# First layer's queries, keys and values of a decoder trunk: one projection in nine chunk pairs, transposed afterwards

## The chip, the core and the metric

One core of one Trainium2 chip runs the whole program. The metric is the device time of one execution in microseconds (us), median of the runs. PE is TensorE (matrix products; PEld its weight loads), DVE is VectorE, ACT is ScalarE, POOL is GpSimd, SP is SyncE, which issues the weight transfers.

## The reference, cut to what matters

The trunk has two layers of different kind, 256 tokens, width 2048, all in float32. What the change touches is the first layer's mixer: 24 heads in three dilation groups (8 columns of heads `j`, three groups `g` each), and four heads that attend to a memory.

```python
def mixer_a(u, mem_n, w_in, w_mem_kv, w_out):
    B, S, _ = u.shape                                # 1, 256, 2048
    na = len(DIL_GROUPS) * A_HEADS_PER_GROUP         # 3 * 8
    proj = u @ w_in                                  # 9216 columns of q, k, v and 512 of mq
    qkv = proj[..., :3 * na * HEAD_DIM].reshape(B, S, 3, na, HEAD_DIM)
    mq = proj[..., 3 * na * HEAD_DIM:].reshape(B, S, MEM_HEADS, HEAD_DIM)
    o_dil = dilated_attention(qkv[:, :, 0], qkv[:, :, 1], qkv[:, :, 2])
    o_mem = memory_attention(mq, mem_n, w_mem_kv)
    return jnp.concatenate([o_dil.reshape(B, S, -1), o_mem.reshape(B, S, -1)], axis=-1) @ w_out

def swiglu(u, w_gu, w_down):
    gu = u @ w_gu
    return (jax.nn.silu(gu[..., :D_FF]) * gu[..., D_FF:]) @ w_down

for l in range(DEPTH):                               # rmsnorm around each part
    x = x + rmsnorm(mixer(rmsnorm(x, g[0])), g[1])   # mixer_a, then mixer_b
    x = x + rmsnorm(swiglu(rmsnorm(x, g[2]), ffn_w_gu[l], ffn_w_down[l]), g[3])
```

The softmax of a head `j` runs over the keys of its three groups together, with a linear bias by distance.

## The kernel before

**Arithmetic.** Every float32 operand is kept as two parts, `hi` (what the matrix engine takes) and `lo` (the rest), and a product is `hi*hi + lo*hi + hi*lo`. Weights arrive by DMA as `raw` (units of 512 KB, two k-tiles of 512 columns or eight of 128), ACT copies `hi` (line 258), DVE subtracts `lo` (line 259). Activations lie transposed, 16 k-tiles `xT` of 128 features by 256 tokens, both parts side by side.

**Forms of a projection.** In the w-form (`w_unit`, `w_mm`) a 128x128 block of weights is stationary and the tokens stream: one matmul of 512 columns (weight `hi` against both parts, line 390) and one of 256 (weight `lo`, lines 389 and 392) for each k-tile. The result is transposed, features by tokens, as queries and keys are needed. In the x-form (`x_unit`, `x_mm`) the tokens are stationary and the weights stream, three matmuls of the chunk's width; the result is tokens by features, as values are needed.

**Seven products.** `Block7` computes a pair of chunks (2 x 512 columns) for both token tiles. A normal k-pair costs 24 matmuls of 512 columns: step `a` for the first chunk and step `b` for the second, 12 each. A k-pair of kind `S` forms sums of the weights on DVE (steps `T13`, `T24`; lines 274, 275, 284, 285) and uses sums of the activations (`Sx`, `Ex`, made once by `x_sums`), and costs 7 x 3 = 21. The products P1 to P7 are put together by additions on DVE (`add`, line 509). Before, the feed-forward chunks of both layers run in this way, in `gu_pair` and in `dn`.

**The stage that the change rewrites.** For each head column `j` of eight there are six w-form projections (queries and keys of three groups, units `a_qk`, evacuated by `evac_w`, lines 417 to 419: two parts added, times the token norm) and one x-form of 384 columns (`a_v`, lines 425 to 427). Then `a_head` is spawned.

**What sets the order.** Each engine runs its own queue in the order in which the code issues. The main stream of matmuls calls `tick()` after each; at a tick one of the side generators (`spawn`) issues its next piece, and `yield n` puts it off for n ticks. `a_head`, `mem_head`, `x_sums` and the evacuations are such generators, so the `yield` numbers fix where their instructions stand among the main ones. `take` looks ahead by `st["look"]` weight units, keeping `st["res"]` pages free: 4 and 0 in this stage, 5 and 5 in the pairs. `a_head` makes scores (line 704), softmax (709 to 717), nine transposes (727, 734), the product with the values (744, 746), and `put_o` (612, 613), which splits the result into the input `oT` of the output projection.

## Time and profile before

| | us |
|---|---|
| runs, median of 3 | 2511.36 (2510.72 to 2513.29) |
| profiled execution, its own time | 2510.36 |
| its span in the profile | 2508.6 |
| PE busy | 2464.3 (98%) |
| DVE busy | 1975.7 (79%) |
| ACT busy | 1360.5 (54%) |
| queries, keys, values and heads of the first layer | 87.4 to 528.9 |
| output projection of the first mixer | 528.9 to 599.5 |
| first feed-forward layer, first matrices | 625 to 1104 |

Busy time counts what an engine executes; matmuls overlap in it, so the time that one takes in the stream is read from one start to the next. The span ends with the last instruction, and the execution's time includes 1.8 us around it.

### The profile page before, as it was taken

The numbers are of one execution on the slowest core, as the hardware profiler recorded it, in microseconds if no ns is written. First come the engines' busy times: TensorE is split into PE (matmuls) and PEld (weight loads), VectorE is DVE, ScalarE is ACT, GpSimd is POOL, SyncE is SP. The second block draws the span as 40 slices with busy tenths as digits, with TensorE's granted clock in tenths as the row PEclk, the third lists the DMA queues.
The fourth block names the chain that finished last, engine by engine and source line by source line (L and its number), as shares of the span: only waits on it lengthen the run. The fifth ranks groups of instructions, "written<-read, shape, count | busy, mean of one in ns | idle before, by whom it ended". The sixth has DMA issues, their size and how long they took to land.

```text
span 2508.6 us, 33084 instructions
## 1 busy us (share of the span) xinstructions
PE 2464.3 (98%) x12050; PEld 2084.8 (83%) x12050; DVE 1975.7 (79%) x2820; ACT 1360.5 (54%) x1984; POOL 76.6 (3%) x106
## 2 busy tenths in 40 slices
PE   8999999999999999999999999999899999999998
PEld 6899999988888888778888888888778888878886
DVE  8555555557798989898897866895689989899796
ACT  7443444446565556565565556565455555555553
POOL 5000000000000000000000000000000000000000
PEclk9999999999999999999999999999999999999999
DMA  7555555576576655476586566346556656458664
GB/s 280 182 179 172 173 164 171 170 252 219 192 252 209 220 170 194 165 252 221 200 291 206 213 247 211 112 150 226 183 186 222 229 177 209 164 171 286 210 221 151
DMA packets 143140, 508.07 MB, mean 203 GB/s; under 512 B 16224, under 2 KB 16352, under 8 KB 142976
## 3 DMA queue, kind: packets, MB, share of 16 engines
q1 hardware_dynamic: 134208, 476.24, 54.8%
q0 software_dynamic: 8048, 28.61, 3.2%
q8 instruction: 94, 1.54, 0.2%
q10 hardware_dynamic: 720, 1.11, 0.1%
q14 instruction: 70, 0.57, 0.1%
HBM read 491.21 MB, written 14.68 MB: 202 GB/s over the span
## 4 chain that ended last, share of the span: by engine, by line
PE 87%; DVE 7%; ACT 3%; issue 2%; DMA 0%; POOL 0%; SPq 0%; DVEq 0%; ACTq 0%; POOLq 0%
PE bk L467 16%; PE bk L465 16%; PE bk L466 16%; PE bk L390 12%; PE bk L392 6%; PE bk L426 5%; PE bk L427 5%; PE bk L425 5%; DVE lo L259 3%; ACT hi L258 2%; PE sk L1068 1%; PE sk L704 1%; PE bk L1407 1%; PE bk L1406 1%; DVE x L814 0%
## 5 line engine op out<-in xcount | busy, mean ns | idle before, releaser
L259 DVE TENSOR_TENSOR lo<-raw,hi 128x1024 fp32r<-128x1024 f32 (+2 forms) x899 | 1043.7, 1205 | 202.9 <-ACT hi L258 188.7
L258 ACT ACTIVATE hi<-raw 128x1024 fp32r<-128x1024 f32 (+2 forms) x899 | 884.3, 1034 | 90.7 <-DVE raw L285 28.4
L390 PE MATMUL bk<-xT,hi 128*128 128x512 f32 x1104 | 399.3, 405 | 0.0
L465 PE MATMUL bk<-hi,xf 128*128 128x512 f32 x780 | 308.2, 395 | 0.0
L467 PE MATMUL bk<-lo,xf 128*128 128x512 f32 x780 | 304.6, 391 | 0.0
L466 PE MATMUL bk<-hi,xf 128*128 128x512 f32 x780 | 304.3, 390 | 0.0
L392 PE MATMUL bk<-xT,lo 128*128 128x256 f32 x1035 | 289.8, 280 | 0.0
L258 ACT ACTIVATE hi<-t 128x1024 fp32r<-128x1024 f32 x92 | 97.7, 1062 | 278.4 <-DVE t L275 258.6
L390 PEld LDWEIGHTS bk<-xT,hi 128*128 128x128 f32 x1104 | 204.1, 188 | 40.0 <-issue 0.2
L465 PE MATMUL bk<-hi,hT 128*128 128x512 f32 x576 | 224.5, 390 | 0.0
L467 PE MATMUL bk<-lo,hT 128*128 128x512 f32 x576 | 224.1, 389 | 0.0
L466 PE MATMUL bk<-hi,hT 128*128 128x512 f32 x576 | 224.1, 389 | 0.0
L392 PEld LDWEIGHTS bk<-xT,lo 128*128 128x128 f32 x1035 | 195.5, 189 | 3.2
L467 PEld LDWEIGHTS bk<-lo,xf 128*128 128x128 f32 x780 | 146.8, 188 | 31.2
L466 PEld LDWEIGHTS bk<-hi,xf 128*128 128x128 f32 x780 | 147.1, 189 | 29.5
L465 PEld LDWEIGHTS bk<-hi,xf 128*128 128x128 f32 x780 | 147.2, 189 | 29.2
L467 PEld LDWEIGHTS bk<-lo,hT 128*128 128x128 f32 x576 | 108.1, 188 | 22.5
L465 PEld LDWEIGHTS bk<-hi,hT 128*128 128x128 f32 x576 | 108.1, 188 | 22.3
L466 PEld LDWEIGHTS bk<-hi,hT 128*128 128x128 f32 x576 | 108.1, 188 | 22.3
L259 DVE TENSOR_TENSOR lo<-t,hi 128x1024 fp32r<-128x1024 f32 x92 | 112.0, 1218 | 0.0
L418 DVE TENSOR_TENSOR ev<-bk,ev 128x256 f32<-128x256 f32 x93 | 39.3, 422 | 91.7 <-ACT ev L417 90.9
L417 ACT ACTIVATE ev<-bk 128x256 f32<-128x256 f32 x93 | 35.6, 382 | 130.4 <-PE bk L390 130.2
(303 smaller groups left out, 4376.9 us busy)
## 6 DMA issues: line engine op xcount, KB each, us to landing
raw<-in_gu SPq DMA_DIRECT2D x352, 512.0 KB, 4.6
raw<-in_dn SPq DMA_DIRECT2D x176, 512.0 KB, 4.5
raw<-in_a_qk SPq DMA_DIRECT2D x96, 512.0 KB, 3.2
raw<-in_a_v SPq DMA_DIRECT2D x64, 384.0 KB, 3.1
raw<-in_cw SPq DMA_DIRECT2D x32, 512.0 KB, 4.6
raw<-in_b_out SPq DMA_DIRECT2D x32, 512.0 KB, 3.6
raw<-in_a_out SPq DMA_DIRECT2D x24, 512.0 KB, 3.8
raw<-in_b_q SPq DMA_DIRECT2D x24, 512.0 KB, 3.2
```

The source lines that it names most:

```text
L258: nc.scalar.activation(hi, src, AF.Copy)
L259: nc.vector.tensor_tensor(out=lo, in0=src, in1=hi.bitcast(F32), op=OP.subtract)
L390: mm(pt[:, :], lhsT=hi[:, ks], rhs=X.hl(kt), start=first, stop=last)
L392: mm(pt[:, S:], lhsT=lo[:, ks], rhs=X.part(kt, 0), start=False, stop=False)
L417: nc.scalar.activation(t1, pt[1][:, S:], AF.Copy)
L418: nc.vector.tensor_tensor(out=t1, in0=pt[1][:, :S], in1=t1, op=OP.add)
L425: mm(p[:, :w], lhsT=xh, rhs=u[0][1][:, ws], start=f, stop=False)
L426: mm(p[:, :w], lhsT=xl, rhs=u[0][1][:, ws], start=False, stop=False)
L427: mm(p[:, :w], lhsT=xh, rhs=u[1][1][:, ws], start=False, stop=l)
L465: mm(p, lhsT=xh, rhs=wh, start=f, stop=False)
L466: mm(p, lhsT=xl, rhs=wh, start=False, stop=False)
L467: mm(p, lhsT=xh, rhs=wl, start=False, stop=e)
```

## The change

The 9216 columns of queries, keys and values become one x-form projection `a_in`, in 18 chunks of 512, in nine pairs by `Block7`, with three `S` k-pairs and five normal ones in each. Its columns are ordered by head: three blocks of 128 for the queries, three for the keys, three for the values. What `gu_pair` did is moved into a common `x_pair`, which the feed-forward calls with its own closing part (`after`); its order of work is as before. After each pair, `a_after` scales the results on ACT by the token norm (values straight into their place, queries and keys in place), transposes the 128x128 pieces of queries and keys on PE, four at most in a group, and copies them on ACT to `aq` and `ak`; when a head's last value block is there, it spawns `a_head`. `x_sums` is issued during the memory queries. `a_head` takes one PSUM bank at a time, and banks are given back six ticks later (`later`).

```diff
+A_PAIRS = 9
+A_QUADS = range(3)
@@ the list of weight units
-    for j in range(AH):
-        u += [("a_qk", j * 12 + i) for i in range(12)]
-        u += [("a_v", j * 8 + i) for i in range(8)]
+    u += _a_order()
@@ x_pair, the common part of gu_pair
+    def x_pair(name, plan, X, Sx, Ex, end, after):
...
+        def evac():
+            yield 10
+            (s1, u2), (u3, v) = T["c"]
+            blk.add("P2", s1, s1)
+            blk.add("P5", v, u3, False)
+            blk.add("P5", u2, u2)
+            yield 1
+            blk.add("P4", u3, u3)
+            blk.add("P3", u2, u2)
+            yield from after(T["c"])
@@ a_head
-            bk = yield from sbank(1 + t)
...
+            for gs in ((0, 1, 2),) if t == 0 else ((0, 1), (2,)):
+                (sb_, s), = yield from sbank()
+                for i, g in enumerate(gs):
+                    mm(s[:, i * n:(i + 1) * n], lhsT=q[1][:, g, t * P:(t + 1) * P], rhs=k[1][:, g, :n], start=True, stop=True)
+                yield 3
...
+                later(sb_)
+                yield 1
@@ put_o and the transposes of a_head
-        banks.put(b)
+        later(b)
@@ the mixer's stage
+    Sx, Ex = {}, {}
+    spawn(x_sums(Xu, Sx, Ex))
     for h in range(4):
         pt = proj_w("a_mq", Xu)
         if h == 0:
-            drain()
+            until(lambda: "R" in rx)
...
+    def a_after(cp):
+        def run(c):
+            tr, done = [], []
+            for i in range(2):
...
+                    for t in range(2):
+                        x, r = c[t][i][:, n * P:(n + m) * P], rx["rs" if kd == 0 else "r"][:, t:t + 1]
+                        nc.scalar.activation(e[kd][1][:, t, g * P:(g + m) * P] if kd == 2 else x, x, AF.Copy, scale=r)
...
+                yield 3
+            yield 4
+            while tr:
+                now, tr = tr[:2], tr[2:]
+                (b, p), = yield from sbank()
+                for f, (_, _, i, n) in enumerate(now):
+                    for t in range(2):
+                        nc.tensor.transpose(p[:, f * S + t * P:f * S + (t + 1) * P], c[t][i][:, n * P:(n + 1) * P], ident)
+                yield 2
...
+                later(b)
+                yield 2
+            for j in done:
+                spawn(a_head(j, *(hd[j][kd] for kd in range(3)), O, 4 + j))
+    for cp in range(A_PAIRS):
+        if cp == 2:
+            until(lambda: O.done.issuperset(range(4)))
+            free_mem(0)
+        x_pair("a_in", _x_steps(A_QUADS), Xu, Sx, Ex, cp == A_PAIRS - 1, a_after(cp))
```

Lines of the changed kernel are shifted: `lo` is line 273 there, the weight sums 288 to 299, `put_o` 712 and 713, `add` 523, the pair's matmuls 479 to 481, a head's value product 840 and 842, the scaling 1075, the transposes 1088.

**The order on VectorE around a head's end.** Before, `put_o` (`oT`) of a head stands among the weight splits and the evacuation (`ev`) of a projection:

```order
L259 TENSOR_TENSOR lo_2526<-raw_2400,hi_2525 128x1024
L259 TENSOR_TENSOR lo_2565<-raw_2422,hi_2564 128x1024
L613 TENSOR_TENSOR oT_624<-sk_2584,oT_624 128x256
L418 TENSOR_TENSOR ev_2595<-bk_2524,ev_2595 128x256
L419 TENSOR_TENSOR aq_2392<-ev_2595,Rs 128x256
L259 TENSOR_TENSOR lo_2601<-raw_2473,hi_2600 128x1024
L259 TENSOR_TENSOR lo_2623<-raw_2502,hi_2622 128x1024
```

In the changed kernel, at the border from one pair to the next, `put_o` of a head is followed by weight splits, the five rows of a seven-product k-pair (`hl`, `t`, `raw`) with its `lo`, and the additions `ut`, of which the first three of five are shown:

```order
L713 TENSOR_TENSOR oT_623<-sk_2087,oT_623 128x256
L273 TENSOR_TENSOR lo_2097<-raw_2015,hi_2096 128x1024
L273 TENSOR_TENSOR lo_2103<-raw_2033,hi_2102 128x1024
L273 TENSOR_TENSOR hl_2120<-raw_2039,hl_2120 128x512
L288 TENSOR_TENSOR t_354_2123<-raw_2039,raw_2033 128x512
L289 TENSOR_TENSOR t_354_2123<-raw_2039 128x512
L298 TENSOR_TENSOR raw_2033<-t_354_2123,raw_2033 128x512
L299 TENSOR_TENSOR raw_2033<-raw_2033 128x512
L273 TENSOR_TENSOR lo_2143<-t_354_2123,hi_2142 128x1024
L523 TENSOR_TENSOR ut_2057<-bk_1707,ut_2057 128x512
L523 TENSOR_TENSOR ut_2058<-bk_1821,ut_2058 128x512
L523 TENSOR_TENSOR ut_2057<-bk_1821,ut_2057 128x512
```

What reads the value product of a head is now ahead of the additions in the same queue.

**The order on PE at the same place.** Before, a head's value product (`apT`, `apU` against `av`) stands between main matmuls, and nothing on PE reads a result of that time soon after:

```order
L392 MATMUL bk_2022<-xT_16_96,lo_1917 128x256
L744 MATMUL sk_2082<-apT_2037,av_1390 128x256 x3
L746 MATMUL sk_2082<-apU_2038,av_1390 128x128 x3
L389 MATMUL bk_2022<-xT_16_96,lo_1917 128x256
L390 MATMUL bk_2022<-xT_16_96,hi_1916 128x512
```

In the changed kernel the value product of that head is followed by 45 main matmuls (two shown at either end) and then by the first group of transposes, which read the sums `ut`:

```order
L840 MATMUL sk_2087<-apT_2044,av_1392 128x256 x3
L842 MATMUL sk_2087<-apU_2045,av_1392 128x128 x3
L479 MATMUL bk_1817<-hi_1999,ex_1090 128x512
L480 MATMUL bk_1817<-hi_1999,ex_1090 128x512
...
L480 MATMUL bk_2128<-hi_2035,xT_14_94 128x512
L481 MATMUL bk_2128<-lo_2036,xT_14_94 128x512
L1088 MATMUL sk_2184<-cst,ut_2057 128x128
L1088 MATMUL sk_2184<-cst,ut_2058 128x128
L1088 MATMUL sk_2184<-cst,ut_2057 128x128
L1088 MATMUL sk_2184<-cst,ut_2058 128x128
```

The transposes are new on PE, and they stand at a fixed distance behind the value product.

**The order on VectorE in the memory queries' stage.** Before, a memory head's maximum (`nm`) and reciprocal (`rec`) stand among `put_o` of another head, weight splits and the evacuations of queries:

```order
L259 TENSOR_TENSOR lo_834<-raw_701,hi_833 128x1024
L259 TENSOR_TENSOR lo_863<-raw_723,hi_862 128x1024
L627 TENSOR_REDUCE nm<-sk_874 128x2
L636 RECIPROCAL rec<-den 128x2
L638 TENSOR_SCALAR mp_882<-mp_882,rec 128x256 x2
L613 TENSOR_TENSOR oT_621<-sk_893,oT_621 128x256
```

In the changed kernel the rows of `x_sums` (`sv`, `xw`, `sx`) stand between:

```order
L677 TENSOR_TENSOR sv<-xw_766 128x128
L678 TENSOR_TENSOR sv<-sv,xw_766 128x128
L679 TENSOR_TENSOR sv<-xw_766 128x128
L680 TENSOR_TENSOR sv<-xw_766,sv 128x128
L684 TENSOR_TENSOR sx_794<-sv,sx_794 128x4x128
L273 TENSOR_TENSOR lo_812<-raw_660,hi_811 128x1024
L673 TENSOR_TENSOR xw_830<-xT_12_92 128x512
L727 TENSOR_REDUCE nm<-sk_834 128x2
L689 TENSOR_TENSOR sv<-xw_830 128x256
L713 TENSOR_TENSOR oT_621<-sk_853,oT_621 128x256
L736 RECIPROCAL rec<-den 128x2
```

The same steps of a memory head are on this engine's queue, with six or seven rows of `x_sums` between one head's and the next.

## Rows read from the trace of the kernel before

**Rows 1.** The page: busy time of each engine with its share of the span and its count of instructions, and the chain of work that ended last, by engine.

```profile
PE 2464.3 (98%) x12050; PEld 2084.8 (83%) x12050; DVE 1975.7 (79%) x2820; ACT 1360.5 (54%) x1984; POOL 76.6 (3%) x106
...
PE 87%; DVE 7%; ACT 3%; issue 2%; DMA 0%; POOL 0%; SPq 0%; DVEq 0%; ACTq 0%; POOLq 0%
```

**Rows 2.** The table by stretches, one for each of the eight heads of the stage that is rewritten (first, last and sum). Columns: stretch and length in us, then busy us (count) of PE, PEld, DVE, ACT, POOL, the granted PE clock, DMA share, GB/s.

```profile
87.40:142.60 55.20, 55.20 (x316) 50.36 (x316) 30.60 (x46) 24.08 (x41) 0.00 (x0) 1.00 0.52 172
...
473.69:528.87 55.18, 55.18 (x323) 50.61 (x323) 30.85 (x45) 24.22 (x37) 1.67 (x3) 1.00 0.60 198
sum 441.47, PE 441.47 PEld 404.69 DVE 246.66 ACT 193.63 POOL 1.67; mean PE 55.18 PEld 50.59 DVE 30.83 ACT 24.20 POOL 0.21
```

**Rows 3.** The timeline of PE in one head: a head's small matmuls and the main matmul that resumes behind each. Columns: start in us, duration, engine, line, out<-in, sizes, count (a float32 matmul leaves two records).

```profile
201.08 0.83 PE L704 MATMUL sk<-ak,aq 128*128 128x128 f32 x6
201.66 0.47 PE L390 MATMUL bk<-xT,hi 128*128 128x512 f32 x1
201.98 0.28 PE L392 MATMUL bk<-xT,lo 128*128 128x256 f32 x1
...
204.18 1.46 PE L704 MATMUL sk<-ak,aq 128*128 128x256 f32 x6
205.29 0.58 PE L390 MATMUL bk<-xT,hi 128*128 128x512 f32 x1
...
212.42 0.49 PE L727 MATMUL sk<-cst,ap 128*128 128x128 f32 x3
212.66 0.48 PE L390 MATMUL bk<-xT,hi 128*128 128x512 f32 x1
...
217.28 1.46 PE L744 MATMUL sk<-apT,av 128*128 128x256 f32 x6
...
219.16 0.36 PE L389 MATMUL bk<-xT,lo 128*128 128x256 f32 x1
```

**Rows 4.** The table by stretches, for one of the middle pairs of the first feed-forward layer (columns as in rows 2); the pair ahead of it and the two behind it differ by 0.01 at most in length and PE.

```profile
787.22:829.64 42.42, 42.42 (x193) 35.14 (x192) 38.65 (x48) 23.64 (x30) 1.06 (x2) 1.00 0.66 226
```

**Rows 5.** The timeline of PE in that pair: two main matmuls, the second 63 places behind the first with no other work between, and a group of four transposes with the main matmul behind it.

```profile
787.21 0.39 PE L465 MATMUL bk<-hi,ex 128*128 128x512 f32 x1
...
801.49 0.39 PE L465 MATMUL bk<-hi,xf 128*128 128x512 f32 x1
...
805.58 0.60 PE L1068 MATMUL sk<-cst,ut 128*128 128x128 f32 x4
805.93 0.48 PE L465 MATMUL bk<-hi,xf 128*128 128x512 f32 x1
```

**Rows 6.** Groups of instructions by line and shape in one head: busy us and mean ns of one.

```profile
L734 PE MATMUL sk<-cst,ap 128*128 128x128 f32 x6 | 1.0, 272 | 0.0
```

**Rows 7.** The timeline of ACT and DVE behind the same value product as in rows 3: `put_o`, the next `hi` and its `lo`. In brackets the idle time ahead and what ended it.

```profile
219.44 0.38 ACT L612 ACTIVATE oT<-sk 128x256 fp32r<-128x256 f32 x1 [2.94 <-PE sk L746]
...
219.86 0.42 DVE L613 TENSOR_TENSOR oT<-sk,oT 128x256 fp32r<-128x256 f32 x1 [2.09 <-ACT oT L612]
...
220.08 2.00 ACT L258 ACTIVATE hi<-raw 128x1024 fp32r<-128x1024 f32 x2
...
221.17 1.22 DVE L259 TENSOR_TENSOR lo<-raw,hi 128x1024 fp32r<-128x1024 f32 x1
```

**Rows 8.** The timeline of DVE, and of ACT in the last row, at the border of two pairs of the first feed-forward layer: two `lo`, a seven-product k-pair, the additions (five in one row), the products with the gate, and the first reading of a sum on ACT.

```profile
791.13 2.35 DVE L259 TENSOR_TENSOR lo<-raw,hi 128x1024 fp32r<-128x1024 f32 x2
793.40 0.68 DVE L259 TENSOR_TENSOR hl<-raw,hl 128x512 fp32r<-128x512 f32 x1
...
795.32 0.69 DVE L284 TENSOR_TENSOR raw<-t,raw 128x512 f32<-128x512 f32 x1
...
796.66 1.22 DVE L259 TENSOR_TENSOR lo<-t,hi 128x1024 fp32r<-128x1024 f32 x1
797.79 3.07 DVE L509 TENSOR_TENSOR ut<-bk,ut 128x512 f32<-128x512 f32 x5
800.79 1.66 DVE L1183 SCALAR_TENSOR_TENSOR ut<-ut,r_f 128x256 f32<-128x256 f32 x4
...
798.51 0.51 ACT L1182 ACTIVATE ut<-ut,r_f 128x256 f32<-128x256 f32 x1 [2.06 <-DVE ut L509]
```

**Rows 9.** Groups of instructions by line on DVE in the first chunks of the feed-forward layer, where `x_sums` runs: the three costliest of its lines, busy us and mean ns of one.

```profile
L1126 DVE TENSOR_TENSOR xw<-xf 128x512 f32<-128x512 f32 x8 | 5.5, 685 | 0.0
L1142 DVE TENSOR_TENSOR sv<-xw 128x256 f32<-128x256 f32 x5 | 2.1, 423 | 0.1
L1137 DVE TENSOR_TENSOR sx<-sv,sx 128x512 fp32r<-128x512 f32 x3 | 2.1, 689 | 1.4 <-ACT sx L1135 1.4
```

**Rows 10.** The table by stretches (columns as in rows 2): the memory queries with what runs ahead of them, the last pair of the first feed-forward layer, and 4 us in that pair.

```profile
58.30:87.40 29.10, 27.59 (x161) 24.05 (x160) 20.28 (x33) 13.45 (x25) 3.06 (x4) 1.00 0.54 201
1060.60:1104.00 43.40, 39.53 (x171) 31.88 (x170) 39.68 (x56) 26.19 (x35) 1.62 (x3) 0.96 0.55 198
1074.00:1078.00 4.00, 4.00 (x11) 3.15 (x12) 4.00 (x5) 2.22 (x3) 0.00 (x0) 0.57 0.45 142
```

**Rows 11.** The timeline of PE in that last pair, ahead of those 4 us.

```profile
1068.90 0.39 PE L467 MATMUL bk<-hl,sx 128*128 128x512 f32 x1
1071.93 0.50 PE L465 MATMUL bk<-hi,sx 128*128 128x512 f32 x1 [2.63 <-ACT hi L258]
...
1073.90 0.50 PE L467 MATMUL bk<-lo,sx 128*128 128x512 f32 x1 [1.24 <-DVE lo L259]
```

More of the change, by code (lines that the diff above doesn't have):

```diff
@@ L518, in common, with sums @@
             self.add("P7", u3, u2)
+    def x_pair(name, plan, X, Sx, Ex, end, after):
+        T = {}
+        blk = Block7(name, X, plan, lambda kt, t: [X.part(kt, i, t * P, (t + 1) * P) for i in range(2)],
+                     lambda u: Sx[u]["s"] if u in Sx else None, lambda kt: Ex.get(kt))
+        st["spare"] = lambda: 7 - len(blk.bk)
+        def sums():
+            yield 12
+            T["pg"] = [pages.get([P, 2, 512], F32, "ut") for _ in range(2)]
+            (s1, u2), (u3, v) = T["c"] = [[e[1][:, j, :] for j in range(2)] for e in T["pg"]]
+            blk.common(s1, u2, u3)
+        def evac():
[8 more added lines that the diff above has]
+            yield from after(T["c"])
+            for e in T["pg"]:
+                pages.put(e[0])
+        st["res"], st["look"] = 5, 5
+        for j, (kd, u) in enumerate(plan):
+            blk.step(kd, u)
+            if kd == "S" and all(e[0] != "S" for e in plan[j + 1:]):
+                spawn(sums())
+            if end and kd != "a":
+                X.drop_one(u)
+                if kd == "S":
+                    pages.put(Sx[u]["pg"][0])
+                elif u == KT // 2 - 1 or (u - GU_E[0]) % 2:
+                    pages.put(Ex[("pg", u - (u - GU_E[0]) % 2)][0])
+        spawn(evac())
     def partial(ssq, n):
@@ L608, in norm, with x_sums, later, wait @@
             res["R"] = yield from bcast(r, name)
+    def x_sums(X, Sx, Ex):
+        e = None
+        for u in range(KT // 2):
+            while not X.done.issuperset((2 * u, 2 * u + 1)):
+                yield 0
+            yield 4
+            x = X.t[u][1].bitcast(F32)
+            i, w = pages.get([P, 2, 2, P], F32, "xw")
+            tt = nc.vector.tensor_tensor
+            tt(out=w.rearrange("p k t q -> p k (t q)"), in0=x[:, :, 0, :], in1=x[:, :, 1, :], op=OP.add)
+            yield 3
+            if u < 3:
+                sv = tmp.tile([P, 4, P], F32, tag="sv", name="sv")
+                tt(out=sv[:, 0], in0=w[:, 1, 1], in1=w[:, 0, 1], op=OP.add)
+                tt(out=sv[:, 1], in0=sv[:, 0], in1=w[:, 0, 0], op=OP.subtract)
+                tt(out=sv[:, 2], in0=w[:, 0, 0], in1=w[:, 0, 1], op=OP.subtract)
+                tt(out=sv[:, 3], in0=w[:, 1, 0], in1=sv[:, 1], op=OP.subtract)
+                pg = pages.get([P, 4, 2, P], F32R, "sx")
+                nc.scalar.activation(pg[1][:, :, 0, :], sv, AF.Copy)
+                yield 3
+                tt(out=pg[1][:, :, 1, :], in0=sv, in1=pg[1][:, :, 0, :].bitcast(F32), op=OP.subtract)
+                Sx[u] = {"pg": pg, "s": [[pg[1][:, j, k, :] for k in range(2)] for j in range(4)]}
+                yield 3
+            if u in GU_E:
+                sv = tmp.tile([P, 4, P], F32, tag="sv", name="sv")
+                tt(out=sv[:, :2], in0=w[:, :, 0], in1=w[:, :, 1], op=OP.subtract)
+                at = (u - GU_E[0]) % 2 * 2
+                if at == 0:
+                    e = pages.get([P, 4, 2, P], F32R, "ex")
+                    Ex[("pg", u)] = e
+                nc.scalar.activation(e[1][:, at:at + 2, 0, :], sv[:, :2], AF.Copy)
+                yield 3
+                tt(out=e[1][:, at:at + 2, 1, :], in0=sv[:, :2], in1=e[1][:, at:at + 2, 0, :].bitcast(F32),
+                   op=OP.subtract)
+                for k in range(2):
+                    Ex[2 * u + k] = [e[1][:, at + k, j, :] for j in range(2)]
+                yield 3
+            pages.put(i)
+    def later(b, n=6):
+        def wait():
+            yield n
+            banks.put(b)
+        spawn(wait())
     def put_o(O, kt, b, p):
@@ L1156, in gu_pair, with after @@
[L1156 to L1179 removed]
+    def gu_pair(l, cp, X, Sx, Ex, H, Sp, rf):
+        def after(c):
+            for i in range(2):
+                H.grow(2 * cp + i)
@@ L1185, in evac @@
             yield 8
-            for c in range(2):
-                yield from gu_split(2 * cp + c, [T["c"][t][c][:, S:] for t in range(2)], H, Sp)
-            for e in T["pg"]:
-                pages.put(e[0])
-        st["res"], st["look"] = 5, 5
-        for j, (kd, u) in enumerate(plan):
-            blk.step(kd, u)
-            if kd == "S" and all(e[0] != "S" for e in plan[j + 1:]):
-                spawn(sums())
-            if cp == GU_PAIRS[-1] and kd != "a":
-                X.drop_one(u)
-                if kd == "S":
-                    pages.put(Sx[u]["pg"][0])
-                elif u == KT // 2 - 1 or (u - GU_E[0]) % 2:
-                    pages.put(Ex[("pg", u - (u - GU_E[0]) % 2)][0])
-        spawn(evac())
+            for i in range(2):
+                yield from gu_split(2 * cp + i, [c[t][i][:, S:] for t in range(2)], H, Sp)
+        x_pair(f"gu{l}", _gu_steps(cp), X, Sx, Ex, cp == GU_PAIRS[-1], after)
     def ffn(l, X, rf, gidx, step=lambda u: None, first=lambda c: None):
```

140 lines of the change are left out of this document (45 added, 95 removed).

## The prediction

> **What bounds the kernel now.** I read the page first: TensorE is busy for 98% of the span and carries 87% of the chain that ended last [rows 1]. Then the table by stretches, for the stage that the change rewrites: eight heads of 55.18 us, 441.47 us in all, with PE busy in every nanosecond, VectorE at 30.8 and ScalarE at 24.2 us of 55.2, the DMA engines at about half [rows 2]. So this stage is matrix work and nothing else, and whatever shortens PE's row shortens the kernel, provided that no wait appears. Last I read how PE's row is spent there [rows 3] and in the first feed-forward layer, where pairs of chunks already run the scheme with seven products [rows 4, 5].
>
> **What PE saves.** One head's own small matmuls take, start to start, 0.58 (first scores), 1.11 (second scores), 0.24 for each of three sets of transposes and 1.88 (values) [rows 3], 4.29 in all. The first main matmul behind a small group costs 0.32 instead of about 0.23 [rows 3]; with six or seven such returns a head's own work is 4.95. Eight of them are 39.6, so the projection itself costs 441.5 - 39.6 = 401.9 now.
>
> After: a pair is 21 matmuls for each of three k-pairs and 24 for each of five, 183 in all, each 512 columns. 63 of them take 801.49 - 787.21 = 14.28 [rows 5], 0.2267 each. A whole pair of the first feed-forward layer, which issues the same 183, takes 42.42 with its two groups of four transposes [rows 4], and a group takes 0.44: 0.35 until the next main matmul starts and 0.09 that this one is slower [rows 5]. 42.42 - 0.88 = 41.54 = 183 x 0.227, so two places agree. Nine pairs: 373.9. New are 96 transposes of queries and keys in 27 groups, at 0.11 each 10.5. The heads' own work stays. Saving: 401.9 - 373.9 - 10.5 = **17.5 us**.
>
> On the transposes a page speaks against the change. By their durations they are not cheap: in this trace a transpose record lasts 272 ns [rows 6], and if they did not overlap, 96 would take 26.1 instead of 10.5. The starts decide: four in 0.35 [rows 5], three in 0.24 [rows 3]. The Trainium skill ("TensorE: Matmul & The Clock Gate", Part 4: PE-mode transpose) gives about 275 ns for one inside a kernel; an estimate by it is 26.4 us and a saving of 1.6. This trace's record agrees with that duration, but its starts do not make it a price, so the sum keeps 0.11.
>
> The bytes are the same, and the DMA engines, at 0.52 here and 0.66 in a feed-forward pair without a gap on PE [rows 2, 4], cost nothing in either.
>
> **What is late next: the border between two pairs.** The results leave PSUM by five VectorE additions, are scaled on ScalarE, and only then transposed. PE executes in its own order, in which 45 main matmuls stand between a head's last value product and the first transposes, 45 x 0.227 + 0.09 = 10.3 us. VectorE's order is fixed too: the head's `put_o`, two `lo`, the five steps of a seven-product k-pair with its `lo`, then the additions. Count from the moment at which main matmuls resume (219.16 in the head shown). ScalarE's copy starts at +0.28, `put_o`'s subtraction at +0.70; the next `hi` is ScalarE's next instruction at about +0.64, and `lo` starts 1.09 after `hi` [rows 7]: +1.73. From there VectorE is back to back, by the durations of the same chain in the feed-forward layer [rows 8]: two `lo` at 1.135 to +4.00, `hl` and the first sums 1.92 to +5.92, two more 1.34 to +7.26, a `lo` 1.13 to +8.39, then five additions of 0.60: P2 at +8.39, P5 +8.99 and +9.59, P4 +10.19, P3 +10.79. ScalarE reads a sum 0.72 after its addition started [rows 8], so the P4 piece can be scaled from +10.91, and PE wants the first group finished at 10.3 + 0.4 = 10.7. In the feed-forward pair nothing like this shows because no head's `put_o` holds the chain back, and the transposes come 3.9 us after their operands [rows 5, 8].
>
> How late depends on how many scalings (0.3 to 0.4 each) stand on ScalarE ahead of those that the first group needs, which differs as the nine chunks of a head fall into pairs of eight. Going through the six borders with a value product just ahead (pairs 2 to 7), the last operand is there at 12.5, 13.0, 13.4, 11.7, 11.8 and 12.4: PE waits 1.8 + 2.3 + 2.7 + 1.0 + 1.1 + 1.7 = **10.6 us**. Bounds: 4, if ScalarE and the hop are 1 us quicker each time; 16, if they are 1 us slower. At the first two borders and the last nothing stands between, and VectorE has 3 to 6 us in hand: nothing.
>
> **The start.** `x_sums` costs VectorE some 15 us, 5.5 in its first line, 2.1 in each of the next two [rows 9], the rest in lines of 0.9 to 1.7. It now runs while the memory heads are made, where VectorE is already busy for 20.28 of 29.1 us [rows 10], and the heads' softmax steps stand behind it. I put 1.2 on the heads' transposes and 0.8 on the rest, **2.0** (bounds 0.5 and 5).
>
> **The end.** The last head's transposes, copies, value product and `put_o` now run with no main matmul between them, since the output projection needs them at once: two hops like that of [rows 7], 0.7 each, **1.4** (0.9 to 3).
>
> **The seven-product steps.** Weights are prepared a little less far ahead here than in the feed-forward pairs. The price when that fails is seen at the end of that layer: PE waits 2.63 and 1.24 us for `hi` and `lo` [rows 11], and the granted clock then falls from 2.4 to 1.2 GHz for some 3 us, 0.57 in the mean of the next four [rows 10]. In the four middle pairs the same plan runs with no gap [rows 4]. Here each `hi` is released at least 6.8 us before its use, by my count along both queues. I take **0.7** for all (0 to 8).
>
> Sum: 17.5 - 10.6 - 2.0 - 1.4 - 0.7 = 2.8 us gained. The profiled execution took 2510.36, so 2507.6; the median of the runs is 1.0 higher, which gives 2508.6.
>
> **The rivals.**
> (a) The border hides. If the transposes find their operands ready as they do in the feed-forward pairs, only start, end and steps are paid: 17.5 - 4.1 = 13.4, 2498. For it speaks the 3.9 us of slack there [rows 5, 8]; against it, the order of both queues behind `put_o`, by which the additions end only at +11.
> (b) The seven-product steps starve, as in the last feed-forward pair of which PE is busy for only 39.53 of 43.40 us, at a mean clock of 0.96 [rows 10]. The head's softmax steps come in bursts between the weight splits, and they take the place of little: the pair has 38.65 of 42.42 us of VectorE work already [rows 4]. At 2 us in each of eight pairs the change loses 16 - 2.8 = 13: 2524. It decides from 1 us a pair on. Against it: with PE at about 48 us per pair, head included, VectorE's share is no higher than in the pairs that run full.
> (c) Transposes that do not overlap, priced above by their records: 15.6 us more, 2524.
> (d) Start and end at their upper bounds, 4.6 more: 2513, no change.
>
> **How the numbers follow.** A measurement of this kernel tells a change from none at about 0.2%, 5.0 us: faster is below 2506.3, slower above 2516.4. The forecast's case has 0.50, and its own spread from 2502 to 2514 lies to about a third on the faster side; (a) 0.16, (b) 0.17, (c) 0.03, (d) 0.14. Faster: 0.16 + 0.18 = 0.34; slower: 0.17 + 0.03 = 0.20, with a hundredth from the forecast's tail 0.21; the rest 0.45. The range has to reach half into (a) and half into (b): 2497 to 2520.
>
> **What would show it.** In the changed kernel's table by stretches, the stage from the first to the last pair near 424 + 15 us, PE not full; pairs of about 47 us plus 1 to 3. On PE, before the first transposes group of pairs 3 to 8 (the evacuation of pairs 2 to 7), an idle time of 1 to 2.7 us released by ScalarE's scaling; none there means (a). Idle time before matmuls that read `sx`, released by `hi` or `lo`, with the clock down behind it, means (b). Groups of four transposes at 0.35 to 0.44 clear (c). The layers behind the output projection should be the same to within 1 us; if they are not, the prediction is wrong outside of its terms.

## The result, and the profile after

The changed kernel takes 2547.0 us (median of four runs, 2544.2 to 2549.9) against 2512.0 before: a ratio of 1.0142 [1.013, 1.0154]. It is 35 us slower, where a gain of 2.8 (2508.6) was forecast, and outside the range of 2497 to 2520. The profiled spans are 2546.8 and 2508.6; the 38.2 between them are what is accounted for here.

The page of the changed kernel, busy time of each engine and the chain that ended last:

```profile
PE 2471.9 (97%) x11489; PEld 2045.2 (80%) x11489; DVE 2104.2 (83%) x2967; ACT 1429.1 (56%) x2081; POOL 79.0 (3%) x106
...
PE 78%; DVE 12%; ACT 5%; issue 3%; DMA 1%; POOL 0%; SPq 0%; DVEq 0%; ACTq 0%; POOLq 0%
```

TensorE issues 561 records fewer than in [rows 1] and is busy for longer; its share of the chain falls from 87% to 78%, and VectorE's rises from 7% to 12%. VectorE is not the bound by its share (83%). It has become something that PE waits for.

The stage, from the first matmul of the memory queries to the first that reads `oT`, in the table by stretches (columns as in rows 2). Before, in one row:

```profile
58.36:528.97 470.61, 469.10 (x2722) 428.79 (x2721) 266.89 (x392) 207.12 (x318) 4.67 (x7) 1.00 0.53 177
```

After, the whole stage, then a pair in which no head runs, then two later ones:

```profile
58.56:560.90 502.34, 472.20 (x2152) 385.94 (x2151) 392.40 (x536) 272.54 (x407) 4.64 (x7) 0.97 0.49 166
...
145.00:192.00 47.00, 47.00 (x215) 38.89 (x214) 40.67 (x49) 27.57 (x37) 0.00 (x0) 1.00 0.54 180
...
254.00:308.00 54.00, 50.51 (x219) 40.70 (x219) 40.99 (x55) 29.25 (x44) 0.00 (x0) 0.94 0.47 156
...
362.00:416.00 54.00, 51.67 (x243) 42.12 (x242) 41.07 (x55) 29.04 (x44) 0.00 (x0) 0.99 0.45 148
```

Where no head runs, PE is full at 2.4 GHz. In the two with heads PE lacks 3.5 and 2.3 us, and the granted clock is below 1. The 38.2 us by place:

| | before | after | us |
|---|---|---|---|
| idle time of PE in the stage | 1.5 | 30.1 | +28.6 |
| busy time of PE in the stage | 469.1 | 472.2 | +3.1 |
| output projection of the first mixer, with the last head's end | 70.5 | 73.1 | +2.6 |
| second layer, from its first `oT` to its feed-forward | 103.4 | 105.9 | +2.5 |
| first matrices of both feed-forward layers | 965.1 | 966.5 | +1.4 |

What PE waited for in the stage (line, what ended the wait; us in all, times, longest):

```profile
PE sk L802 <- DVE ap L805: 14.5, 7, 2.5
PE sk L1088 <- ACT ut L1075: 7.4, 10, 1.3
PE sk L743 <- DVE mp L738: 3.5, 1, 3.5
PE sk L597 <- POOL r_x L657: 3.0, 1, 3.0
...
```

The second row is the border that the prediction was about, the third and fourth are the start. The first row, half of all the idle time, stands in no term of the sum: the last score product of seven heads (line 802, 704 before) waits for the softmax step of the scores ahead of it (line 805).

One of these seven on PE:

```profile
216.75 0.39 PE L481 MATMUL bk<-lo,xT 128*128 128x512 f32 x1
219.56 1.22 PE L802 MATMUL sk<-ak,aq 128*128 128x256 f32 x2 [2.42 <-DVE ap L805]
220.22 0.99 PE L479 MATMUL bk<-hi,xT 128*128 128x512 f32 x1
221.01 0.63 PE L480 MATMUL bk<-hi,xT 128*128 128x512 f32 x1
221.44 0.63 PE L481 MATMUL bk<-lo,xT 128*128 128x512 f32 x1
```

The scores for two groups ran at 212.66, 15 main matmuls followed, and then the third group's scores had to write to a bank that was still being read. Why it was read so late is seen on DVE:

```profile
212.68 0.69 DVE L273 TENSOR_TENSOR hl<-raw,hl 128x512 fp32r<-128x512 f32 x1 [1.36 <-ACT hl L272]
...
215.74 0.69 DVE L299 TENSOR_TENSOR raw<-raw 128x512 f32<-128x512 f32 x1
216.35 1.22 DVE L273 TENSOR_TENSOR lo<-t,hi 128x1024 fp32r<-128x1024 f32 x1
217.62 1.23 DVE L273 TENSOR_TENSOR lo<-raw,hi 128x1024 fp32r<-128x1024 f32 x1
218.76 0.74 DVE L805 SCALAR_TENSOR_TENSOR ap<-mask,sk 128x256 f32<-128x256 f32 x2
```

From 212.68 to 218.76 VectorE worked without a pause through a seven-product k-pair's sums (some rows left out above), splits of weights that PE wants only later, and the end of the softmax of the tile before. The reading of the scores stood behind all of it. Behind the wait main matmuls start 0.43 apart instead of 0.23.

At the border, the pattern that was forecast: PE's last main matmul, the first transposes, and the next group 4.2 us later.

```profile
247.46 0.39 PE L481 MATMUL bk<-lo,xT 128*128 128x512 f32 x1
249.16 0.95 PE L1088 MATMUL sk<-cst,ut 128*128 128x128 f32 x4 [1.31 <-ACT ut L1075]
249.87 0.48 PE L479 MATMUL bk<-hi,xT 128*128 128x512 f32 x1
...
253.38 0.60 PE L1088 MATMUL sk<-cst,ut 128*128 128x128 f32 x4
253.73 0.48 PE L479 MATMUL bk<-hi,xT 128*128 128x512 f32 x1
```

### The profile page after: what moved, and what is told of

The parts are those of the page before. It is cut to its first block, busy times and chain, and to the rows that moved or that the text cites. A ratio compares the mean times of both kernels' runs of the same rounds, so it can differ in the third digit from the quotient of the medians.

```text
span 2546.8 us, 32172 instructions
## 1 busy us (share of the span) xinstructions
PE 2471.9 (97%) x11489; PEld 2045.2 (80%) x11489; DVE 2104.2 (83%) x2967; ACT 1429.1 (56%) x2081; POOL 79.0 (3%) x106
## 4 chain that ended last, share of the span: by engine, by line
PE 78%; DVE 12%; ACT 5%; issue 3%; DMA 1%; POOL 0%; SPq 0%; DVEq 0%; ACTq 0%; POOLq 0%
PE bk L481 19%; PE bk L479 19%; PE bk L480 18%; DVE lo L273 5%; PE bk L404 5%; PE bk L440 3%; PE bk L439 3%; PE bk L441 3%; ACT hi L272 3%; PE bk L406 2%; DVE ut L523 1%; PE sk L1203 1%; DVE hl L273 1%; PE bk L1470 1%; PE bk L1469 1%
## 5 line engine op out<-in xcount | busy, mean ns | idle before, releaser
L273 DVE TENSOR_TENSOR lo<-raw,hi 128x1024 fp32r<-128x1024 f32 (+1 forms) x883 | 1041.9, 1223 | 162.4 <-ACT hi L272 149.1
L272 ACT ACTIVATE hi<-raw 128x1024 fp32r<-128x1024 f32 (+1 forms) x883 | 881.8, 1049 | 102.9 <-DVE raw L299 34.7
L272 ACT ACTIVATE hi<-t 128x1024 fp32r<-128x1024 f32 x119 | 126.2, 1061 | 326.1 <-DVE t L289 303.9
L273 DVE TENSOR_TENSOR lo<-t,hi 128x1024 fp32r<-128x1024 f32 x119 | 145.0, 1218 | 1.4 <-ACT hi L272 1.4
L479 PE MATMUL bk<-hi,xT 128*128 128x512 f32 x351 | 145.6, 415 | 0.0
L481 PE MATMUL bk<-lo,xT 128*128 128x512 f32 x351 | 139.9, 399 | 0.0
L480 PE MATMUL bk<-hi,xT 128*128 128x512 f32 x351 | 139.6, 398 | 0.0
L523 DVE TENSOR_TENSOR ut<-bk,ut 128x512 f32<-128x512 f32 x203 | 129.1, 683 | 2.8 <-ACT ut L529 1.3
L404 PE MATMUL bk<-xT,hi 128*128 128x512 f32 x336 | 126.8, 416 | 0.0
L479 PE MATMUL bk<-hi,ex 128*128 128x512 f32 x290 | 115.5, 398 | 0.0
```

What stands on the lines that cost most here:

```text
L272: nc.scalar.activation(hi, src, AF.Copy)
L273: nc.vector.tensor_tensor(out=lo, in0=src, in1=hi.bitcast(F32), op=OP.subtract)
L404: mm(pt[:, :], lhsT=hi[:, ks], rhs=X.hl(kt), start=first, stop=last)
L479: mm(p, lhsT=xh, rhs=wh, start=f, stop=False)
L480: mm(p, lhsT=xl, rhs=wh, start=False, stop=False)
L481: mm(p, lhsT=xh, rhs=wl, start=False, stop=e)
```

## The experiments

Three theories. **The distance:** the wait belongs to the score products, which stand too close to their reader, and a longer distance cures it. **The bank:** the pair reserves seven of the eight PSUM banks (`st["spare"] = lambda: 7 - len(blk.bk)`), so the head has one for its scores, its transposes, its value product and the border's transposes, and each use waits for the reader of the use before; lengthen one distance and another use pays. **The queue (Q):** what makes the reader late is the order on VectorE and ScalarE, where splits for later weights stand ahead of it; with fewer of them ahead, one bank is enough. A fourth, rival V in the expectations, is VectorE's work as a whole: whatever the order, PE would idle as long. The times below are medians, against 2547.0 for the changed kernel; each ratio is to the kernel before on the same chip.

**1. Twenty ticks between the two score groups.**

```diff
-        yield 8
+        yield 2
         for t in range(2):
...
-                yield 1
+                yield 20 if t == 1 and gs == (0, 1) else 1
...
-        yield 13
+        yield 7
```

> Theory S (the score bank): the changed kernel loses most where the last group of a head's scores waits for VectorE to have read the group before it, whose PSUM bank it takes. PE idles there for 1.7 to 2.6 us in each of seven heads, 15.6 us in all, and the granted clock is down behind the longer of these waits, about 1.6 us more in each pair. Here that group stands 33 to 36 main matmuls behind the first instead of 15; the head's first wait is shortened, so that its value product stays about 45 matmuls ahead of the transposes as it was. Theory S expects the waits of the scores gone or under 0.5 us, the clock at 1.00 in the later pairs, and 2547 - 22 to 27 = about 2522. Rival T (the transposes at the border set the time and the scores only absorb slack): the waits move to the transposes, and the time stays within 5 us of 2547. Rival V (VectorE is the bound): the same idle time turns up at the next matmul that reads a weight split, 2540 or more.

Measured: 2545.3, 1.0132 [1.0115, 1.0148]. The waits of line 802 are gone from PE's list, and the same sum stands at another line, the transposes of the probabilities (line 830), released by ScalarE's copy of the product P1 (line 529), which gives back one of the pair's banks:

```profile
PE sk L830 <- ACT ut L529: 16.8, 7, 3.9
```

A miss for the forecast, and the distance theory falls in the form that asks only for more room between the scores: the wait is not the scores' own.

**2. The border's transposes later, the head's start earlier.**

```diff
-        yield 8
+        yield 2
...
-        yield 13
+        yield 11
...
-            yield 4
+            yield 12
             while tr:
```

> The border term of the prediction alone: the first transposes of a pair stand 57 main matmuls behind the head's value product instead of 45, 2.7 us later; the scores are where they were. In the changed kernel these transposes wait 9.5 us in all. If they wait for the scaling on ScalarE and nothing else, that is gone and the time falls to about 2537.5. If VectorE is simply late by a fixed share, the wait moves on to the next groups and to the scores, and the time stays within 3 us of 2547. Theory S expects the waits of the scores unchanged, 15 us in all.

Measured: 2541.8, 1.0122 [1.0107, 1.0137], between the two forecasts; the interval overlaps with that of the changed kernel. The border's own wait can be moved away at once (7.4 in the changed kernel, 1.1 now), and that of the scores falls to 10.8, but most of this is paid at the transposes of the probabilities (line 830: 8.5 us in three rows, the third of 0.9 not shown; 1.0 in the changed kernel):

```profile
PE sk L802 <- DVE ap L805: 10.8, 7, 2.1
PE sk L830 <- DVE ap L813: 4.3, 3, 1.5
...
PE sk L830 <- DVE ut L523: 3.3, 6, 1.2
...
PE sk L1088 <- ACT aq L1092: 1.1, 1, 1.1
```

**3. The activation sums behind the memory queries.**

```diff
-    spawn(x_sums(Xu, Sx, Ex))
     for h in range(4):
...
+    spawn(x_sums(Xu, Sx, Ex))
     hd = [{} for _ in range(AH)]
```

> The sums of the activations are issued behind the last memory query instead of ahead of the first. In the changed kernel PE waits 3.2 us for the token norm (1.7 before), 3.6 us for a memory head's softmax, 0.5 for another, and the clock is down behind the two long ones, 4 us more. If it is the sums on VectorE's queue that make these late, the stretch falls by 7 to 9 us, to about 2539, unless the first pair's seven-product steps now wait for the sums, which would take back 2 to 6 and show as idle time ahead of matmuls that read sx in the first pair. If the memory heads are late for another reason (the bank, the new weight sums of pair 0), nothing changes: 2546.

Measured: 2554.2, 1.0169 [1.0154, 1.0184], 7 us slower than the changed kernel, a miss for the forecast of 2539; its exception, that the first pair waits for the sums, is what happened. The two waits at the start fall to 1.5 each (3.0 and 3.5 in the changed kernel), and the first pair waits for the sums themselves:

```profile
PE bk L479 <- ACT ex L694: 4.3, 2, 2.7
PE bk L480 <- DVE ex L696: 2.0, 1, 2.0
PE sk L597 <- POOL r_x L657: 1.5, 1, 1.5
PE sk L743 <- DVE mp L738: 1.5, 1, 1.5
```

So the later place is too late for the first seven-product step; that VectorE's time ahead of that step is what the start lacks is tested in experiment 5.

**4. Score distance, sums behind, and the value product behind the border's transposes.**

```diff
-                yield 1
+                yield 20 if t == 1 and gs == (0, 1) else 1
...
-        yield 5
+        yield 40
         (ob, o), = yield from sbank()
...
-    spawn(x_sums(Xu, Sx, Ex))
     for h in range(4):
...
+    spawn(x_sums(Xu, Sx, Ex))
```

> All together, in a form that may beat both kernels: the last group of scores 33 to 36 matmuls behind the first, the value product behind the border's transposes instead of ahead of them (so that no put_o stands ahead of the additions), and the sums issued behind the memory queries. If the three causes add up (22 to 27, 9.5, 7 to 9), about 2505, faster than before (2512). If the waits only move, above 2520. Rival V expects PE to idle at weight splits in every pair and at least 2530.

Measured: 2537.4, 1.0107 [1.0092, 1.0122]. Better than experiments 1 and 3 (the moved value product was not run alone), still 26.5 us behind the kernel before on the same chip: of the two forecasts the one for waits that only move (above 2520) holds, not 2505. The value product (line 840) now waits 5.0 us for a reading of the next head's scores, another use of the same bank.

**5. The first pair without seven products, the sums behind the memory queries.** The first pair is made of four plain chunk halves (192 matmuls instead of 183), so that no sum is needed until the second.

```diff
+    def plain_pair(after):
+        pts = [[bank(), bank()] for _ in range(2)]
+        for u in range(KT // 2):
+            for p in pts:
+                x_unit(p, "a_in", Xu, 2 * u, 512, u == 0, u == KT // 2 - 1)
...
     for cp in range(A_PAIRS):
+        if cp == 0:
+            plain_pair(a_after(0))
+            continue
```

> The first of the nine pairs is made without seven products (192 matmuls of 512 columns instead of 183, 2.0 us more), so that the sums of the activations, issued behind the memory queries, have a whole pair to be made in and nothing waits for them; the other eight pairs are as in the changed kernel. Theory: the start costs about 10 us because fifteen us of sums are pressed in ahead of someone who needs them, the memory heads in the changed kernel, the first pair with the sums moved behind (that run was 8 us slower). Then all these waits go, of 3.2, 3.6 and 0.5 us beyond the 1.7 that the kernel before had, with 4 us of low clock behind them: 2547 - 10 + 2 = 2539. Rival (VectorE is behind for the whole stage, and the start only shows it first): the waits come back in the second pair, 2545 or more.

Measured: 2540.3, 1.0117 [1.01, 1.0134], as expected. The stretch from 87.4 to 150 us has no gap and the full clock, where the changed kernel had 59.13 us of PE at 0.95:

```profile
87.40:150.00 62.60, 62.60 (x288) 52.01 (x287) 45.34 (x74) 35.60 (x60) 0.00 (x0) 1.00 0.39 139
```

The stage falls from 502.3 to 492.0 us although it has nine matmuls more (2.0 us), 12.3 in all. 10.4 of this is there by the first transposes behind the second pair (they start 136.3 us into the stage in the changed kernel, 127.9 here): this is what the start had cost, clock included. The rest lies in later pairs, where the waits are the same (14.6 us at the scores, 7.5 at the border) but the granted clock fell four times instead of six.

**6. The seven-product steps at the pair's beginning,** one behind each of the first three steps, so that a pair's later part has more banks free; with the distances of the first experiment.

```diff
+def _a_steps():
+    std = [u for u in range(KT // 2) if u not in A_QUADS]
+    o = []
+    for i, u in enumerate(std):
+        o.append(("a", u))
+        if i < len(A_QUADS):
+            o.append(("S", A_QUADS[i]))
+    return o + [("b", u) for u in std]
```

> Same as the run with the late last scores (2545), but the three seven-product k-pairs of each pair stand behind the first, second and third step instead of the fourth, fifth and sixth or so: same matmuls, same VectorE work, same places of the head's work among the matmuls. What changes is that the seven open products occupy seven of the eight PSUM banks until about matmul 117 of the pair instead of 165, so the transposes of the probabilities and the value product no longer have to share one bank. Theory B (one bank is left, and each use of it waits for its reader, whose queue is behind): the 18 us of waits at these transposes vanish with the low clock behind them, 2545 - 18 to 27 = about 2522. Rival V (VectorE's total work is the bound): the same idle time, at weight splits or elsewhere, 2540 or more; or worse, since the sums of weights now come in a burst.

Measured: 2562.2, 1.0202 [1.0186, 1.0217], the slowest of all. The 16.8 us that the first experiment had at line 830 are gone altogether, as the bank theory says. But the pair's own products now wait for banks that the pair before has not yet given back, and so do the border's transposes for theirs:

```profile
PE bk L489 <- DVE ut L533: 13.8, 10, 2.2
PE sk L1098 <- ACT ak L1102: 4.9, 2, 3.2
...
PE sk L1098 <- ACT ak L1105: 3.4, 1, 3.4
...
```

In the memory heads at the start PE also waits 9.2 us (4.3, 3.8 and 1.1), against 4.3 in the first experiment. The forecast time was a miss; that the waits are waits for a bank is shown twice over, by those that went and by those that came.

**7. In the second layer, `put_o` gives its bank back at once.**

```diff
-        later(b)
+        if len(O.t) == 6:
+            later(b)
+        else:
+            banks.put(b)
```

> Only put_o in the second layer gives its PSUM bank back at once, as in the kernel before; everything in the first layer is as in the changed kernel. The changed kernel is 2.5 us longer in the second layer's output projection stretch (105.9 against 103.4 us), with a wait of 2.4 us of a head's scores for ScalarE. If that is the late return of the bank, the stretch is 103.4 again and the time 2544.5; if it is something else (the order in which banks went round since the first layer), nothing changes.

Measured: 2542.0, 1.0125 [1.011, 1.014]. This is 5.0 below the changed kernel, but the intervals of the two ratios overlap; the stretch is the surer measure. The stretch before the second feed-forward is back at 103.4 us. The changed kernel waits there once, which neither the kernel before nor this one does:

```profile
PE sk L1577 <- ACT pcT L1635: 2.3, 1, 2.3
```

So `later` in the common `put_o`, six ticks more for one bank, cost the second layer 2.5 us.

**8. Experiments 5, 6 and 7 together** (the edits shown there).

> The first pair without seven products, the seven-product steps early, the last scores late, put_o in the second layer as before. If start (8), banks (25) and second layer (2.5) add up: 2547 - 35 = 2512, equal to the kernel before, with the border's transposes (up to 9 us) as what is left. Rival V: above 2530.

Measured: 2552.5, 1.0162 [1.0147, 1.0177], a miss for the forecast: 10 better than experiment 6, about what the plain first pair and `put_o` gave by themselves, while the 13.8 us for `ut` stay and the border's transposes wait 17.5.

**9. Fewer splits ahead, other places.** Experiments 5 and 7 with the order of steps of the changed kernel, `look` 3 instead of 5 in this projection, and new distances.

```diff
-        st["res"], st["look"] = 5, 5
+        st["res"], st["look"] = 5, (3 if name == "a_in" else 5)
...
-                yield 1
+                yield 6 if t == 0 else 1
...
-        yield 13
+        yield 18
...
-        yield 5
+        yield 12
         (ob, o), = yield from sbank()
...
-            yield 4
+            yield 8
             while tr:
```

> A version meant to beat both kernels. First pair without seven products and put_o of the second layer as before (both measured alone, 7 and 2.5 us better), and in the other eight pairs two things: weights are split for three units ahead instead of five, and the head's pieces stand a little elsewhere among the main matmuls (second scores 3 matmuls later, transposes of the probabilities 9 later, the value product 18 later, the border's transposes 6 later). The last group of scores stays 15 matmuls behind the group whose bank it takes. Theory Q (the readers are late because weight splits for steps that are still far off stand ahead of them in VectorE's and ScalarE's queues): the waits of scores and transposes go, the clock stays up, and with the saving of 17.5 us less 2.0 for the plain first pair and some 5 left over the time is about 2502, ratio about 0.996. If only the places in PE's order count, the waits of the last scores stay at 2 us a head and the time is about 2525. If three units ahead are too few, PE idles at hi and lo in every pair: above 2520.

Measured: **2499.3 (2498.3 to 2500.5), 0.9952 [0.994, 0.9965]**: faster than both kernels, with the same single bank. The stage in the table by stretches, and all that is left of waits in it of a microsecond or more:

```profile
58.30:512.30 454.00, 452.59 (x2149) 376.79 (x2148) 372.47 (x507) 265.70 (x401) 4.81 (x7) 1.00 0.54 182
```

```profile
PE sk L598 <- POOL r_x L658: 1.4, 1, 1.4
```

VectorE is busy for 372.5 of 454.0 us here and was for 375.6 of 492.0 in experiment 5, which asks the same of it: its work as a whole is not the bound, and rival V is out.

**10. The same with `look` 5.** Only the order of the splits on ACT and DVE, and of the transfers on SP, differs from experiment 9; on PE all 11498 records stand in the same order in both traces.

```diff
-        st["res"], st["look"] = 5, (3 if name == "a_in" else 5)
+        st["res"], st["look"] = 5, 5
```

> The tuned version with the splits five units ahead again. PE's order is the same, instruction by instruction; only VectorE's and ScalarE's queues differ, in which up to two more units of weight splits stand ahead of a head's rows. Theory Q: the waits come back, at the last scores, at the transposes of the probabilities or at the border, some 10 us and with them the low clock: about 2515, 10 to 16 us behind the tuned version. If the order on PE alone decides, this one equals the tuned version.

Measured: 2511.8, 1.0003 [0.9994, 1.0012], 12.6 us more than experiment 9, all of it in the stage (466.7 against 454.0). The wait of the changed kernel is back:

```profile
PE sk L806 <- DVE ap L809: 8.2, 4, 2.6
```

One of the four on VectorE, from the split ahead of the first tile's maximum (`nm`) to the reading of the scores (line 809):

```profile
257.65 1.22 DVE L274 TENSOR_TENSOR lo<-raw,hi 128x1024 fp32r<-128x1024 f32 x1
258.79 0.55 DVE L813 TENSOR_REDUCE nm<-ap 128x1 f32<-128x384 f32 x1
261.06 1.22 DVE L274 TENSOR_TENSOR lo<-raw,hi 128x1024 fp32r<-128x1024 f32 x1 [1.73 <-ACT hi L273]
262.20 0.16 DVE L816 RECIPROCAL rec<-den 128x1 f32<-128x1 f32 x1
262.39 0.42 DVE L817 TENSOR_SCALAR ap<-ap,rec 128x384 f32<-128x384 f32 x1
262.73 0.75 DVE L809 SCALAR_TENSOR_TENSOR ap<-mask,sk 128x256 f32<-128x256 f32 x2
```

And the same place in experiment 9:

```profile
255.92 1.22 DVE L274 TENSOR_TENSOR lo<-t,hi 128x1024 fp32r<-128x1024 f32 x1 [0.40 <-ACT hi L273]
257.06 0.16 DVE L816 RECIPROCAL rec<-den 128x1 f32<-128x1 f32 x1
257.25 0.42 DVE L817 TENSOR_SCALAR ap<-ap,rec 128x384 f32<-128x384 f32 x1
257.59 0.75 DVE L809 SCALAR_TENSOR_TENSOR ap<-mask,sk 128x256 f32<-128x256 f32 x2
```

The scores had been issued on PE at 256.49 in experiment 10 and at 254.48 in experiment 9, so their reading came 6.2 us behind them in the one and 3.1 in the other. In the row with 1.73 VectorE is not even busy: it waits for a `hi` that ScalarE has behind the head's exponential, and the softmax waits behind VectorE. Late transfers are out as a rival: behind the memory queries VectorE and ScalarE wait for a DMA for 0.2 us in experiment 10 and not at all in 9. Theory Q holds at these places: the bank is the same, PE's order is the same, and the order of the two other queues is worth 12.6 us.

**11. `look` 3 with the places of the changed kernel.** The four distances of experiment 9 go back to 1, 13, 5 and 4.

> The tuned version with the head's pieces and the border's transposes at the places of the changed kernel (yields 1, 13, 5 and 4), splits three units ahead. Theory Q alone (only the queue counts): equal to the tuned version. If the places count as well, because the one bank is asked for again before any reader could be done, waits of about 2 us a head remain: near 2535, no better than the run with the plain first pair (2540) less the 2.5 of put_o.

Measured: 2538.6, 1.0108 [1.0092, 1.0123]; the stage takes 493.3 us.

```profile
PE sk L806 <- DVE ap L809: 24.1, 7, 4.3
```

So theory Q alone, which forecast the time of experiment 9, fails, and fewer splits ahead do not help by themselves: with the old distances a whole seven-product chain lands ahead of the reading (from 259.81 to 264.20 in one head, six rows of it). The border's waits are gone here, those of the scores are larger. The places are the larger part. At `look` 3 they are worth 39 us. At `look` 5 they are worth about 26: no run has the old places with both other edits, but experiment 5 less the 2.5 of `put_o` gives 2537.8 as an estimate for it, and experiment 10 takes 2511.8, as much as the kernel before. `look` 3 is worth 12.6 at the new places and, by the same estimate, nothing at the old.

## Why the prediction was wrong

**The step that failed** is one sentence in the paragraph on what PE saves: "The heads' own work stays." The matmuls of a head do stay; their banks do not. Before, a head took its two score groups' banks at once (`sbank(1 + t)`); the changed kernel passes one bank from use to use. I gave each border its walk through VectorE's queue and did not give it to the other uses of the same bank. The list of waits prices that at 14.5 us, 7 times 2.1, and experiments 1, 2, 4 and 6 show that a single distance pushes it to another use. All places set anew leave 8.2 of it (experiment 10), and with fewer splits ahead as well nothing is left (experiment 9).

**The granted clock** adds about half to what the waits cost. I used its fall only in the rare case of a starving step [rows 10, 11], so the sum has nothing for it. Here the mean of 0.97 over 502.3 us is 15 us by the rounded figure (13 to 18), against 30.1 us of idle time. Of this, 0.94 over the first 86.4 us is 5 us, behind the two long waits at the start; the other 10 lie where heads run, behind waits of the scores and of the border.

**The saving was somewhat smaller than forecast.** With almost no waits left, in experiment 9, the busy time of the stage falls from 469.1 to 452.6 with nine matmuls more (2.0), 18.5 in all. But 3.9 of this has only moved into the stretch behind the stage (100.1 us busy instead of 96.2). The stage and that stretch together, before and in experiment 9:

```profile
58.39:625.27 566.88, 565.37 (x3172) 508.48 (x3171) 333.15 (x492) 259.87 (x407) 9.58 (x16) 1.00 0.55 186
...
58.55:613.52 554.97, 552.78 (x2620) 459.43 (x2618) 443.31 (x613) 322.60 (x501) 9.51 (x16) 1.00 0.55 190
```

That is 12.6 and the nine matmuls, 14.6 against 17.5 forecast. Where the 2.9 went, no run separated. The pair without heads is full at 47.00 of 47.00. A group of four transposes still takes 0.35 (253.38 to 253.73 above), so rival (c) is out. The Trainium skill ("TensorE: Matmul & The Clock Gate", Part 4: PE-mode transpose) gives about 275 ns for a transpose inside a kernel, for bf16; one of this group, in float32, lasts 272 in the trace, and four of them stand within 350.

**The border was right, and nearly to the microsecond.** By starts, with 0.23 and 0.11 as the undisturbed distances, PE loses 1.8, 2.2, 2.7, 1.0, 1.1 and 1.7 at the six borders, 10.5 in all; 10.6 was forecast (1.8, 2.3, 2.7, 1.0, 1.1, 1.7). Rival (a) is out. Of this the list counts 7.4 as idle; the rest lies in the transposes that start one by one.

**The start was mis-sized.** 2.0 was taken, 5 was the bound, and experiment 5 measures 10.4 for it: 5.4 of idle time beyond that of the kernel before, and 5 of low clock. The heads' softmax (3.5) and the token norm, which one instruction of POOL computes from a VectorE result (3.0 against 1.5 before), both stood behind `x_sums`.

**The end** took 0.7 of waiting against 1.4; the other 1.9 of the 2.6 is work of the last head that now stands behind the stage. **The seven-product steps** were right at next to nothing: no wait of the list has `hi` or `lo` as its releaser, so rival (b), whose time (2524) is on the right side, is wrong in its mechanism.

**Outside of the terms:** "the layers behind the output projection should be the same to within 1 us" failed by 2.5 in the second layer. I had read `later` in `put_o` as a step of the first layer; the second calls the same function. The 1.4 us more in the feed-forward layers' first matrices (965.1 to 966.5) are spread: with the same code there, the other runs have 964.9 to 967.8.

The sum with measured sizes: 14.6 saved. Against it stand 28.6 of idle time in the stage (14.5 scores, 7.4 border, 5.4 start, 1.3 others) and 19.6 of busy time beyond that of experiment 9 without its nine matmuls (15 for the clock, 3.1 for the border's transposes that start one by one; the last 1.5 no run separated). With 0.7 for the end, 2.5 and 1.4 for the other layers this gives the 38.2 of the spans. The scores and the clock, for which the forecast had no term, are 30 of these 53 us against.

## What to carry to other kernels

When a change takes PSUM banks from a side task, list every use of the banks that are left and follow each one's reader through its engine's queue; the distance on PE that hides a reader is the work ahead of it in that queue, not its own duration. Set all the distances by that work together, since moving one moves the wait to the next use, and then look for lookahead work in the readers' queues. Here the new places were worth about 26 us (an estimate, as one of its two ends was not run), three units ahead instead of five another 12.6, and the plain first pair and `put_o` some 9: together they turned 1.4% slower into 0.5% faster. And count on the clock behind PE's waits: here it added half as much again.

## What the runs showed of the hardware

A wait of PE can be followed by some 3 us at 1.2 GHz instead of 2.4, with main matmuls 0.43 apart instead of 0.23, which costs some 1.5 us more than the wait itself. The length of that one wait does not tell whether it will be. Four stretches of 3 us, with the granted clock as the third figure from the right; the first three are of the changed kernel, behind a wait of 1.31 at the border, behind one of 2.42 at the scores, and from 1.65 us behind the start of another border's transposes, which had also waited 1.31. The last is of experiment 5, behind a wait of 2.50 at the scores:

```profile
249.10:252.10 3.00, 2.86 (x14) 2.31 (x15) 0.00 (x0) 3.00 (x8) 0.00 (x0) 1.00 0.13 20
...
219.50:222.50 3.00, 2.94 (x7) 2.37 (x8) 2.97 (x5) 0.00 (x0) 0.00 (x0) 0.50 0.68 212
304.60:307.60 3.00, 3.00 (x9) 2.34 (x8) 1.35 (x2) 3.00 (x5) 0.00 (x0) 0.50 0.38 117
...
425.20:428.20 3.00, 2.99 (x13) 2.51 (x14) 2.97 (x4) 0.00 (x0) 0.00 (x0) 1.00 0.78 266
```

So 1.31 us was followed by either level, and 2.4 to 2.5 us too. In experiment 10 a wait of 1.82 left the clock at 1.00 and one of 2.57 was followed by 0.50; in experiment 11 one of 2.69 left it at 1.00. I had expected the fall only behind pairs of waits such as those of [rows 11]; single waits are enough at times, and what decides, no run here shows.
